# One full-array product for both heads' new state in a chunked RWKV-7 scan

## The chip, the cores and the metric

The kernel runs on one core of a Trainium2 chip, in one launch. The metric is device time in microseconds (us): the median of several runs, lower is better. The engines are TensorE (PE in the profile, with its weight loads as PEld), VectorE (DVE), ScalarE (ACT), GpSimd (POOL) and SyncE (SP), which here only issues DMAs.

## What is computed

One block of a streaming encoder over an input of 2048 frames by 1024 channels, float32. The normalised input is projected; its columns feed an RWKV-7 branch of 16 heads by 64, an S5 state-space branch, gates and merge gates. The part that matters here is the RWKV-7 recurrence:

```python
def frame_step(S, inp):
    r_t, w_t, k_t, v_t, a_t, b_t = inp
    sa = jnp.einsum('bhij,bhj->bhi', S, a_t)
    S = S * w_t[:, :, None, :] + sa[..., None] * b_t[:, :, None, :] + v_t[..., None] * k_t[:, :, None, :]
    return S, jnp.einsum('bhij,bhj->bhi', S, r_t)
```

It runs over 2048 frames for each head. The kernel does it in chunks of 64 frames.

## The kernel before

**Units and chunks.** A unit is a pair of heads `p` (8 pairs) and a block `tb` of 512 frames (4 blocks): 32 units, each of 8 chunks of 64 frames, so 256 chunks. The two heads of a pair lie on partitions 0 to 63 and 64 to 127 (`HS[0]`, `HS[1]`).

**A chunk in `scan`.** The tile `su[:, c]` (the profile calls it `SU`) is 128x128 and is the chunk's `cur`. On entry its diagonal 64x64 blocks hold the states of the two heads; the off-diagonal blocks hold the chunk's values, put there ahead by `prep2`: rows 64 to 127 of head 0's columns, rows 0 to 63 of head 1's. A chunk has three stages, with a `yield` between them:

1. `px` (L943): one product of 128x128 by 128 columns over both heads at once; DVE copies it to `rh`, ACT scales the old states into `us` (L948).
2. `po`, first half (L952): the states' part of the output, one product for each head on 64x64. `pu` (L955): the solved correction, one for each head on 64x64. It is scaled into `cur`, in place of the states: DVE writes head 0's diagonal block, ACT head 1's (L957).
3. `pn` (L961): the new state, one product for each head with weights `bt[:, c, h]` of 128x64 and the head's 64 columns of `cur`. DVE adds the decayed old state to it for each head (L969, and L72 for the one that goes through the helper `Woven`) and writes the diagonal block of the next chunk's tile. `po`, second half (L971): the rest of the output, one product for each head with weights `cur[:, HS[h]]` of 128x64; it has the same shape on the array as `pn`.

The weights `bt` are a tile of 8 chunks by 2 heads by 64 columns, made in `prep2`, so that the two heads' columns lie side by side. Products in f32 are two instructions each in the profile, a first and a second pass, each with a weight load.

**The order of the work.** The order on every engine is the order in which the code is written out; nothing is rescheduled. The main loop has 24 slots for each unit. Each slot takes one stage of `scan` for unit n, one piece of the preparation of later units (`prep1`, `prep2`), of `post1`, `sums` and `post2` for earlier ones, and then a share of `gm`, the stream of projections: six matmuls of 128x128 by 512 columns to a piece (L499 to L501, in f32 split into a high and a low part). So in TensorE's queue a chunk's stage stands between groups of projection matmuls, and after them come `pn` and `po` together. DVE's queue holds, beside the scan's steps, the splits of weights, the shifts of the projections, and the solve (L881, L885), which is woven in between other instructions.

**The run as a whole.** The scan fills some 140 to 2064 us of the run; the S5 branch, the GLU and the output projections follow.

Of the kernel before, what the change touches and what calls it, by code (L numbers as in the profile page):

```python
# [13 lines left out]
ALU = mybir.AluOpType  # L14
# [3 lines left out]
P = 128  # L18
# [5 lines left out]
C = 64  # L24
# [54 lines left out]
def tile_rwkv7_s5_block(  # L79
# [32 lines left out]
    pe, act, pool, sp = nc.tensor, nc.scalar, nc.gpsimd, nc.sync  # L112
    raw_dve = nc.vector
    dve = Woven(raw_dve)
    x = x[0]
    out = out[0]
# [34 lines left out]
    for i in range(2):  # L151
        for j in range(2):
            pool.affine_select(
                out=amask[64 * i:64 * i + 64, j, :], in_=amask[64 * i:64 * i + 64, j, :],
# [107 lines left out]
    if True:  # L262
# [14 lines left out]
        HS = (slice(0, 64), slice(64, 128))  # L277
# [656 lines left out]
        def scan(p, tb):  # L934
            n = f"_{p}_{tb}"
            u = U[p, tb]
            ar, at, r64, bt, decs, dd, su = (u[k] for k in ("ar", "at", "r64", "bt", "dec", "dd", "su"))
            po = u["po"] = pso.tile([P, TB], F32, tag="o", name="po" + n)
            for c in range(NC):
                dec = decs[:, c, :]  # L940
                cur = su[:, c, :]
                px = pst.tile([P, 512], F32, tag="st", name=f"px{n}_{c}")
                pe.matmul(px[:, 0:P], at[:, c, 0].rearrange("p h t -> p (h t)"), cur, start=True, stop=True)  # L943
                rh = sm.tile([P, P], F32, tag="rh", bufs=1, name=f"rh{n}_{c}")
                dve.tensor_copy(rh, px[:, 0:P])
                us = sm.tile([P, C], F32, tag="us", name=f"us{n}_{c}")
                for h in range(2):
                    act.activation(out=us[HS[h]], in_=cur[HS[h], HS[h]], func=AF.Copy, scale=dec[HS[h]])  # L948
                yield
                oc = po[:, c * C:(c + 1) * C]  # L950
                for h in range(2):
                    pe.matmul(oc[HS[h]], cur[HS[h], HS[h]], ar[HS[h], c, C:2 * C], start=True, stop=False)  # L952
                pu = pst.tile([P, 512], F32, tag="st", name=f"pu{n}_{c}")
                for h in range(2):
                    pe.matmul(pu[HS[h], 0:C], r64[HS[h], c, :], rh[HS[h], HS[h]], start=True, stop=True)  # L955
                dve.tensor_scalar(out=cur[0:64, 0:64], in0=pu[0:64, 0:C], scalar1=dd[0:64, c:c + 1], scalar2=None, op0=ALU.mult)
                act.activation(out=cur[64:128, 64:128], in_=pu[64:128, 0:C], func=AF.Copy, scale=dd[64:128, c:c + 1])  # L957
                yield
                pn = pst.tile([P, 512], F32, tag="st", name=f"pn{n}_{c}")
                for h in range(2):  # L960
                    pe.matmul(pn[HS[h], 0:C], bt[:, c, h, :], cur[:, HS[h]], start=True, stop=True)  # L961
                for h in range(2):
                    if c + 1 < NC:
                        nxt = su[HS[h], c + 1, HS[h]]
                    elif tb % 2 == 0:
                        nxt = U[p, tb + 1]["su"][HS[h], 0, HS[h]]
                    else:
                        nxt = ust[HS[h], p, :]
                    (raw_dve if h == 0 else dve).scalar_tensor_tensor(out=nxt, in0=pn[HS[h], 0:C], scalar=dec[HS[h]], in1=us[HS[h]], op0=ALU.mult, op1=ALU.add)  # L969
                for h in range(2):  # L970
                    pe.matmul(oc[HS[h]], cur[:, HS[h]], at[:, c, 1, h, :], start=False, stop=True)  # L971
                yield
# [559 lines left out]
        with tc.manual_schedule():  # L1532
# [13 lines left out]
            for n in range(-1, NU + 1):  # L1546
                credit = OFF if n == 0 else credit if n > NU - 2 else 0.0
                sc = scan(*units[n]) if 0 <= n < NU else none
                p2 = prep2(*units[n + 1]) if n + 1 < NU else none
                a = units[n + 2] if n + 2 < NU else None  # L1550
# [337 lines left out]
```

## Time and profile before

| | |
|---|---|
| Time, median of 3 runs | 2669.6 us (2667.75 to 2674.17) |
| The profiled execution | 2672.18 us, span 2670.3 us, granted clock 0.989 |
| PE busy | 2585.2 us (97%) |
| DVE busy | 1824.8 us (68%) |
| ACT busy | 1356.0 us (51%) |
| POOL busy | 536.5 us (20%) |

The span is the time from the first to the last instruction. The profile's groups put together instructions of one line, engine and shape; a form such as `128*64 128x64` is weights of 128 rows by 64 columns, and 128 partitions by 64 columns streamed past them. The rows of the timeline have a start in us from the span's beginning, a length in us and the instruction; neighbours of the same kind are merged, with their number behind the x. The end of a matmul is modelled, so lengths overlap; the distance between two starts is what a step costs. Where a row ends in brackets, the engine stood idle before it for so long, until the named instruction was done.

### The profile page before, as it was taken

To read this page: it belongs to the slowest core of one execution; us is meant where nothing else is said; L and a number is where in the kernel's file an instruction comes from. 1 tells how busy PE (TensorE), PEld (TensorE's weight loads), DVE (VectorE), ACT (ScalarE), POOL (GpSimd) and SP (SyncE) were. 2 spreads that over 40 slices of the span, in tenths; PEclk is the share of its full clock that TensorE was granted. 3 is DMA by queue.
4 is the path that set the end of the run, shared out by engine and by line. 5 is a ranking of instruction groups with operands and counts; after the bars stand their busy time and mean duration, and the time that the engine had idled before them with its cause. 6 is when DMAs were issued, how large, how long until landed. Compare 5 with 4: busy or idle time off the path is not lost.

```text
span 2670.3 us, 48574 instructions
## 1 busy us (share of the span) xinstructions
PE 2585.2 (97%) x17164; PEld 1969.7 (74%) x17164; DVE 1824.8 (68%) x5512; ACT 1356.0 (51%) x3441; POOL 536.5 (20%) x918
## 2 busy tenths in 40 slices
PE   7999999999999989999999999999989699999998
PEld 5777777777777767777777777777767488787887
DVE  6656677777667777767776767777767787554443
ACT  5455555555555677555555555555643443332111
POOL 2221212122112333221212122121321100210000
PEclk9999999999999999999999999999999799999999
DMA  4232323232333443332323233232465555664442
GB/s 129 77 84 65 101 78 102 69 93 81 86 86 95 136 123 104 98 82 78 91 76 96 78 91 90 79 92 74 145 173 155 166 155 146 205 212 145 140 141 95
DMA packets 255977, 294.58 MB, mean 110 GB/s; under 512 B 159505, under 2 KB 171894, under 8 KB 254710
## 3 DMA queue, kind: packets, MB, share of 16 engines
q1 hardware_dynamic: 212134, 147.80, 20.4%
q0 software_dynamic: 43600, 143.69, 17.6%
q8 instruction: 135, 2.21, 0.4%
q14 instruction: 108, 0.88, 0.1%
HBM read 206.80 MB, written 75.89 MB: 106 GB/s over the span
## 4 chain that ended last, share of the span: by engine, by line
PE 46%; DVE 6%; DMA 5%; issue 2%; ACT 2%; SPq 1%; POOL 0%; DVEq 0%; POOLq 0%; ACTq 0%
PE pout L1787 2%; PE pout L1786 2%; PE pout L1788 2%; PE ppa L499 1%; PE pma L499 1%; PE A L830 1%; PE pn L961 1%; PE ppa L500 1%; PE ppa L501 1%; DMA ce<-cw 1%; PE pma L500 1%; PE po L952 1%; PE pma L501 1%; PE pga L499 1%; PE pr L499 1%
## 5 line engine op out<-in xcount | busy, mean ns | idle before, releaser
L957 ACT ACTIVATE SU<-pu,dd 64x64 f32<-64x64 f32 x256 | 79.0, 309 | 368.1 <-DVE SU L72 276.4
L881 DVE TENSOR_TENSOR TM<-RF,IX 128x60 f32<-128x60 f32 (+24 forms) x992 | 207.3, 209 | 29.4 <-DMA IX<-ld 7.3
L885 DVE TENSOR_TENSOR RF<-RF,TM 128x60 f32<-128x60 f32 (+24 forms) x992 | 206.8, 208 | 27.2
L948 ACT ACTIVATE us<-SU,dec 64x64 f32<-64x64 f32 x512 | 176.4, 345 | 58.4 <-DVE SU L969 51.5
L72 DVE TENSOR_SCALAR SU<-pu,dd 64x64 f32<-64x64 f32 x256 | 69.9, 273 | 139.6 <-PE pu L955 60.6
L969 DVE SCALAR_TENSOR_TENSOR SU<-pn,dec,us 64x64 f32<-64x64 f32 x240 | 65.6, 273 | 117.7 <-PE pn L961 116.2
L72 DVE TENSOR_TENSOR AT<-A,amask 64x256 f32<-64x256 f32 (+1 forms) x256 | 102.2, 419 | 62.0 <-PE A L830 41.0
L835 ACT ACTIVATE AT<-A,dd 64x64 f32<-64x64 f32 x512 | 116.5, 302 | 46.6 <-PE A L830 41.4
L961 PEld LDWEIGHTS pn<-SU,BT 128*64 128x64 f32 x1024 | 55.9, 135 | 109.2 <-issue 39.5
L952 PEld LDWEIGHTS po<-AR,SU 64*64 64x64 f32 x1024 | 49.8, 131 | 94.8 <-issue 81.6
L72 DVE COPY rh<-px 128x128 f32<-128x128 f32 x256 | 74.1, 289 | 63.9 <-PE px L943 59.1
L499 PE MATMUL ppa<-yhi,whi_pa 128*128 128x512 f32 x256 | 116.3, 454 | 0.0
L943 PEld LDWEIGHTS px<-SU,AT 128*128 128x128 f32 x512 | 95.3, 189 | 27.1 <-DVE SU L72 6.2
L499 PE MATMUL pmb<-hhi,whi_mb 128*128 128x512 f32 x256 | 111.2, 435 | 0.0
L499 PE MATMUL pk<-hhi,whi_k 128*128 128x512 f32 x256 | 111.1, 434 | 0.0
L499 PE MATMUL pma<-hhi,whi_ma 128*128 128x512 f32 x256 | 111.1, 434 | 0.0
L499 PE MATMUL pga<-hhi,whi_ga 128*128 128x512 f32 x256 | 110.9, 433 | 0.0
L499 PE MATMUL pr<-hhi,whi_r 128*128 128x512 f32 x256 | 110.2, 430 | 0.0
L499 PE MATMUL pv<-hhi,whi_v 128*128 128x512 f32 x256 | 109.8, 429 | 0.3 <-ACT carry L452 0.3
L500 PE MATMUL ppa<-ylo,whi_pa 128*128 128x512 f32 x256 | 104.8, 409 | 3.0 <-DVE ylo L72 3.0
L961 PE MATMUL pn<-SU,BT 128*64 128x64 f32 x1024 | 94.5, 246 | 12.1 <-DVE SU L72 10.1
L501 PE MATMUL ppa<-yhi,wlo_pa 128*128 128x512 f32 x256 | 103.5, 404 | 0.6 <-DVE wlo_pa L72 0.6
(474 smaller groups left out, 7802.9 us busy)
## 6 DMA issues: line engine op xcount, KB each, us to landing
IX<-ld SPq DMA_DIRECT2D x128, 128.0 KB
raw_mb<-in_w_in_dram POOLq DMA_DIRECT2D x50, 256.0 KB, 3.7
raw_pa<-in_p_a_dram POOLq DMA_DIRECT2D x44, 256.0 KB, 3.9
raw_r<-in_w_in_dram POOLq DMA_DIRECT2D x36, 256.0 KB, 3.8
raw_k<-in_w_in_dram POOLq DMA_DIRECT2D x36, 256.0 KB, 4.0
raw_v<-in_w_in_dram POOLq DMA_DIRECT2D x36, 256.0 KB, 3.4
raw_ga<-in_w_in_dram POOLq DMA_DIRECT2D x34, 256.0 KB, 3.5
ce<-cw SPq DMA_DIRECT2D x16, 514.0 KB
```

The source lines that it names most:

```text
L72: r = f(*a, **kw)
L499: pe.matmul(ps, hi[:, k, :], xhi[:, kk_, :], start=(kk_ == 0), stop=False)
L500: pe.matmul(ps, hi[:, k, :], xlo[:, kk_, :], start=False, stop=False)
L501: pe.matmul(ps, lo[:, k, :], xhi[:, kk_, :], start=False, stop=(kk_ == 7))
L835: act.activation(out=at[HS[h], c, 0, h, :], in_=pas[h][HS[h], i, 0:C], func=AF.Copy, scale=dd[HS[h], c:c + 1])
L881: raw_dve.tensor_tensor(out=tm[:, 0:na, 0:nt], in0=rf[:, 0:na, s:s + 1].to_broadcast([P, na, nt]), in1=ix[:, s:s + 1, s + 1:32].to_broadca ...
L885: raw_dve.tensor_tensor(out=rf[:, 0:na, s + 1:32], in0=rf[:, 0:na, s + 1:32], in1=tm[:, 0:na, 0:nt], op=ALU.add)
L943: pe.matmul(px[:, 0:P], at[:, c, 0].rearrange("p h t -> p (h t)"), cur, start=True, stop=True)
L948: act.activation(out=us[HS[h]], in_=cur[HS[h], HS[h]], func=AF.Copy, scale=dec[HS[h]])
L952: pe.matmul(oc[HS[h]], cur[HS[h], HS[h]], ar[HS[h], c, C:2 * C], start=True, stop=False)
L957: act.activation(out=cur[64:128, 64:128], in_=pu[64:128, 0:C], func=AF.Copy, scale=dd[64:128, c:c + 1])
L961: pe.matmul(pn[HS[h], 0:C], bt[:, c, h, :], cur[:, HS[h]], start=True, stop=True)
```

## The change

The two products of `pn` become one. Its weights are both heads' columns of `bt` (128x128), and the whole `cur` is streamed past them, 128 columns. Of the 128x128 result the diagonal blocks are the new states; the two blocks off the diagonal, each head's weights with the other head's columns, are computed and not read. The DVE updates read the diagonal blocks, head 1's now 64 columns further on. `px`, `pu` and both parts of `po` are as before.

```diff
                 pn = pst.tile([P, 512], F32, tag="st", name=f"pn{n}_{c}")
-                for h in range(2):
-                    pe.matmul(pn[HS[h], 0:C], bt[:, c, h, :], cur[:, HS[h]], start=True, stop=True)
+                pe.matmul(pn[:, 0:P], bt[:, c].rearrange("p h k -> p (h k)"), cur, start=True, stop=True)
                 for h in range(2):
...
-                    (raw_dve if h == 0 else dve).scalar_tensor_tensor(out=nxt, in0=pn[HS[h], 0:C], scalar=dec[HS[h]], in1=us[HS[h]], op0=ALU.mult, op1=ALU.add)
+                    (raw_dve if h == 0 else dve).scalar_tensor_tensor(out=nxt, in0=pn[HS[h], HS[h]], scalar=dec[HS[h]], in1=us[HS[h]], op0=ALU.mult, op1=ALU.add)
                 for h in range(2):
                     pe.matmul(oc[HS[h]], cur[:, HS[h]], at[:, c, 1, h, :], start=False, stop=True)
```

On TensorE's queue, at the second chunk of the first unit, where the two heads' products stand between projections and `po`, it was:

```order
L500 MATMUL pga_0_1578<-hlo_179,whi_ga_0_1428 128x512
L501 MATMUL pga_0_1578<-hhi_178,wlo_ga_0_1429 128x512
L961 MATMUL pn_0_1_1614<-SU_0_1011,BT_0_950 64x64 [waits DVE_49]
L961 MATMUL pn_0_1_1614<-SU_0_1011,BT_0_950 64x64 [waits Activation_49]
L971 MATMUL po_0_1414<-AT_0_881,SU_0_1011 64x64 x2
L864 MATMUL pv_1_1622<-cen,zv_0_845 128x128 [waits PE_49]
```

And it is now, with lines one lower:

```order
L500 MATMUL pga_0_1577<-hlo_179,whi_ga_0_1428 128x512
L501 MATMUL pga_0_1577<-hhi_178,wlo_ga_0_1429 128x512
L960 MATMUL pn_0_1_1613<-SU_0_1011,BT_0_950 128x128 [waits Activation_49]
L970 MATMUL po_0_1414<-AT_0_881,SU_0_1011 64x64 x2
L864 MATMUL pv_1_1620<-cen,zv_0_845 128x128 [waits PE_49]
```

Head 0's product waited for DVE and head 1's for ACT; the one product waits for ACT, whose write of head 1's block stands behind DVE's write of head 0's. `po` keeps its place directly behind it. No other instruction moves on any engine.

## The prediction

> **What bounds the kernel now.** First the page's busy times, then the same by stretch (columns: stretch, its length, busy time of PE, weight loads, DVE, ACT and POOL with counts, granted clock, DMA share, GB/s).
>
> ```profile
> PE 2585.2 (97%) x17164; PEld 1969.7 (74%) x17164; DVE 1824.8 (68%) x5512; ACT 1356.0 (51%) x3441; POOL 536.5 (20%) x918
> ```
>
> ```profile
> 140.00:500.00 360.00, 359.12 (x2691) 268.39 (x2689) 250.21 (x836) 204.09 (x571) 75.74 (x128) 1.00 0.31 84
> 500.00:900.00 400.00, 399.54 (x2983) 299.35 (x2980) 285.15 (x960) 227.77 (x577) 88.06 (x151) 1.00 0.33 90
> 900.00:1060.00 160.00, 147.69 (x1079) 107.63 (x1077) 122.60 (x411) 116.58 (x326) 52.36 (x85) 0.99 0.43 122
> 1060.00:1240.00 180.00, 179.30 (x1333) 134.72 (x1332) 125.69 (x417) 102.52 (x301) 42.53 (x73) 1.00 0.33 89
> 1240.00:1710.00 470.00, 469.79 (x3535) 351.35 (x3533) 337.96 (x1117) 267.39 (x686) 97.19 (x169) 1.00 0.30 85
> 1710.00:2064.00 354.00, 343.73 (x2451) 255.03 (x2449) 257.11 (x943) 180.44 (x448) 85.46 (x144) 0.99 0.44 125
> ```
>
> The scan runs from 140 to 2064 us. In four of the six stretches, 1410 us of 1924, PE's rows leave 0.2 to 0.9 us uncovered: there TensorE's fixed order of work is the bound, and a nanosecond more on PE is a nanosecond more of time. Only 900 to 1060 (12.3 us idle) and 1710 to 2064 (10.3 us) have room.
>
> Next, what the changed product is today (groups by form).
>
> ```profile
> L943 PE MATMUL px<-SU,AT 128*128 128x128 f32 x512 | 99.4, 276 | 2.6 <-DVE SU L72 2.6
> L961 PE MATMUL pn<-SU,BT 128*64 128x64 f32 x1024 | 94.5, 246 | 12.1 <-DVE SU L72 10.1
> ```
>
> `pn` has 1024 records, so four for each of 256 chunks: two heads, two passes each. `px` (512, two per chunk) is what `pn` will be: f32, 128x128 weights, 128 columns, the same source tile `SU`. So the new product's price stands in this profile already. Busy times do not give it, because the ends of matmuls are modelled and overlap; starts do. A chunk's end with nothing waited for (columns: start, length, what):
>
> ```profile
> 1023.42 0.40 PE L501 MATMUL pga<-hhi,wlo_ga 128*128 128x512 f32 x1
> 1023.75 0.34 PE L961 MATMUL pn<-SU,BT 128*64 128x64 f32 x4
> 1023.92 0.29 PE L971 MATMUL po<-AT,SU 128*64 128x64 f32 x4
> 1024.13 0.50 PE L499 MATMUL pu<-hhi,whi_u 128*128 128x512 f32 x1
> ```
>
> From the last projection matmul to the next one: 0.71 us. Three things are to be seen. The step into `pn` is 0.33 us. All four passes of `pn` take 0.17 us, as the two heads, on different halves of the columns, run side by side. And `po`, the output product of the same chunk and the same half-array shape, follows with no gap.
>
> **The change part by part.** It removes four passes of 128*64 weights by 64 columns per chunk and adds two of 128*128 by 128 columns. `po` behind it stays on half the array. Nothing else is added; DMAs, ACT and DVE keep their instructions.
>
> *The step in.* The same step into a full-array f32 product:
>
> ```profile
> 1000.87 0.39 PE L501 MATMUL pk<-hhi,wlo_k 128*128 128x512 f32 x1
> 1001.10 0.38 PE L943 MATMUL px<-SU,AT 128*128 128x128 f32 x2
> 1001.24 0.48 PE L499 MATMUL pk<-hhi,whi_k 128*128 128x512 f32 x1
> ```
>
> 0.23 us, against 0.33: the weights are loaded under the projection. Here the change gains 0.10.
>
> *The step out.* After `pn` now comes a product on part of the array. One `px` in the trace is followed by such an operation directly (weights 128*32), and a group of four transposes on the full array is followed by `po` on 64*64:
>
> ```profile
> 2012.72 0.39 PE L501 MATMUL ppa<-yhi,wlo_pa 128*128 128x512 f32 x1
> 2012.95 0.38 PE L943 MATMUL px<-SU,AT 128*128 128x128 f32 x2
> 2013.26 1.05 PE L770 MATMUL sums<-ysq,selr 128*32 128x512 f32 x2
> ```
>
> ```profile
> 1019.83 0.60 PE L315 MATMUL tps<-ident,x 128*128 128x128 f32 x4
> 1020.36 0.33 PE L952 MATMUL po<-AR,SU 64*64 64x64 f32 x4
> ```
>
> 0.31 us from `px`'s first pass to the narrow operation. The transposes say the same: their four rows cover 0.60, the last of them some 0.28 (`px`'s mean), so one starts 0.11 after another, and of the 0.53 up to `po` 0.20 are left for the last step; 0.11 + 0.20 = 0.31. Against 1001.10 to 1001.24 (0.14, when the next operation is on the full array too) the change of shape costs 0.17. Today the pair `pn`, `po` pays that change once on the way in and once on the way out; after the change it pays it between `pn` and `po` and on the way out, so no change of shape is saved.
>
> *`po` alone.* For this a group with a wait in it is of use, where the passes stand apart:
>
> ```profile
> 1006.09 0.67 PE L961 MATMUL pn<-SU,BT 128*64 128x64 f32 x3
> 1006.50 0.27 PE L971 MATMUL po<-AT,SU 128*64 128x64 f32 x1
> 1006.60 0.22 PE L961 MATMUL pn<-SU,BT 128*64 128x64 f32 x1
> 1006.61 0.33 PE L971 MATMUL po<-AT,SU 128*64 128x64 f32 x3
> 1006.87 0.50 PE L499 MATMUL pv<-hhi,whi_v 128*128 128x512 f32 x1
> ```
>
> The first pass after a change of shape takes 0.11 (1006.50 to 1006.61) because its weights lie in the open; later ones take 0.06 (0.17 for `pn`'s two, less 0.11). `pn` and `po` together take 0.38 (1023.75 to 1024.13); without two passes of 0.06 `po` alone takes 0.26.
>
> *Sum for a chunk that waits for nothing:* before 0.33 + 0.38 = 0.71; after 0.23 + 0.31 + 0.26 = 0.80. Starts are rounded to 10 ns, so the loss is 0.08 to 0.11 us; I take 0.095, as the transposes' rows lean a little above. Times 256: **+24.3 us**.
>
> A page weighs in. The Trainium skill, "TensorE: Matmul & The Clock Gate", section "Back-to-back issue gap", gives some 81 ns per matmul of 128 columns for a stream of load and matmul pairs. By it the new product's first pass would take 0.08, not the 0.11 of the rows, and the sum would be some 7 us smaller. The rows decide, since they hold the very operation.
>
> *Chunks that wait.* Both heads now wait for the later half of `SU`: DVE scales the upper half, ACT the lower. In the group above head 0 started at 1006.09; head 1 had to wait for ACT:
>
> ```profile
> 1006.49 0.13 PEld L961 LDWEIGHTS pn<-SU,BT 128*64 128x64 f32 x1 [0.21 <-ACT SU L957]
> ```
>
> It followed 0.40 later, and from there to the projection took 0.38. Afterwards the whole product starts there, and with its weights in the open, as this waiting `px` shows:
>
> ```profile
> 1018.10 0.49 PE L943 MATMUL px<-SU,AT 128*128 128x128 f32 x2 [0.42 <-DVE SU L72]
> 1018.34 0.48 PE L499 MATMUL pga<-hhi,whi_ga 128*128 128x512 f32 x1
> ```
>
> 0.24 instead of 0.14, so 0.10 more: 0.31 + 0.10 + 0.26 = 0.67 against 0.38, a loss of 0.29, which is 0.195 above the loss already counted. How many wait (waits of `pn`'s weight loads: releaser, us, times; the whole run first, then 900 to 1060):
>
> ```profile
>   DVE SU L72: 30.1, 33
>   ACT SU L957: 4.4, 21
> ```
>
> ```profile
>   DVE SU L72: 7.9, 13
>   ACT SU L957: 1.7, 8
> ```
>
> 33 at most: 33 x 0.195 = **+6.4 us**.
>
> *What waits give back.* The first `px` of two successive units of eight chunks:
>
> ```profile
> 1407.52 0.38 PE L943 MATMUL px<-SU,AT 128*128 128x128 f32 x2
> 1465.84 0.38 PE L943 MATMUL px<-SU,AT 128*128 128x128 f32 x2
> ```
>
> 58.32 us for a unit, 7.3 for a chunk. A wait whose end PE does not set shrinks by what PE has lost before it. In the four full stretches there is nothing to shrink. The other two, 514 us, hold some 70 chunks at that pace: 70 x 0.095 = 6.7 us there, and the 6.4 above. Between none and all 13 us comes back; I take **-5**, nearer the low end, because DVE's lateness itself often goes back to an operand that PE made a chunk or two earlier.
>
> *The update behind the product.* DVE's two updates wait for `pn` today:
>
> ```profile
> L969 DVE SCALAR_TENSOR_TENSOR SU<-pn,dec,us 64x64 f32<-64x64 f32 x240 | 65.6, 273 | 117.7 <-PE pn L961 116.2
> 1008.80 0.39 PE L943 MATMUL px<-SU,AT 128*128 128x128 f32 x2
> ```
>
> In a chunk without waits the result ends 0.67 after the last projection start today (1023.75 + 0.34 less 1023.42) and 0.61 afterwards (by `px`, 1001.10 + 0.38 less 1000.87), so slightly earlier: nothing. In a waiting one it ends 0.49 after 1006.49 instead of 0.33, and both updates, 0.27 each, stand behind it: done near 1007.6, with `px` of the next chunk at 1008.80, behind a projection. DVE's queue loses 0.4 us there 33 times at 68% busy. I cost it at nothing; the cover is those six projection matmuls, and where it is gone, `px` is late next.
>
> *Sum:* 24.3 + 6.4 - 5 = +25.7. The profiled execution took 2672.2 us (2670.3 of it the span), which gives 2697.9; the median of the runs is 2.6 below that execution, so **2695**.
>
> **The rivals.**
> *The step out is free (faster).* If `po`'s weights were loaded under `pn`'s second pass, the step from the second pass to `po` would be 0.06, and a chunk would take 0.23 + 0.11 + 0.06 + 0.26 = 0.66: 0.05 x 256 = 12.8 less, 2657. It decides from a step below about 0.10. The Trainium skill's page on TensorE has a rule for it (Part 2, step by step: weight loads are pulled ahead of matmuls in flight where they go to the background buffer); its page "TensorEngine Tiling (Array Packing)", Key Properties, says that a change of mode drains the array. The row at 2013.26 and the one at 1020.36 have 0.20. Chance 0.05.
> *The waits give all of it back (no change).* All of `pn`'s waits for `SU` are 34.5 us, enough in sum. Against it stands the steady part, where PE has 0.2 us free in 470. It would end at 2670 to 2677. Chance 0.07.
> *More chunks come to wait (slower still).* One wait on the later head, and both updates behind one product, lengthen the chain from chunk to chunk by 0.4 us where it is tight. Were 66 more chunks to wait, three times today's number, 66 x 0.195 = 13 would come on top: 2708. For it: heads are 0.40 apart when DVE is late. Against: 223 of 256 chunks do not wait for a half of `SU` today, and the product's result comes no later in them. Chance 0.12.
>
> **How the numbers follow.** The forecast, a loss on every chunk with a little given back, has 0.74; what is left, 0.02, is for the unforeseen on either side. Its own range: 186 chunks in the full stretches at 0.08 give +15 (2685), everything at 0.11 with no wait giving back gives 28 + 6 = +34 (2704). Taking in part of the third rival and some of the second: 2683 to 2707. A measurement here tells 0.3%, 8 us. Slower 0.87, same 0.07, faster 0.06.
>
> **What the profile after would show.** Right: `pn` as 512 records of 128*128 by 128; projection to `pn` 0.23, `pn` to `po` 0.31, `po` to projection 0.26; a unit in the steady part at 58.32 + 8 x 0.095 = 59.1 us; busy time of DVE and ACT unchanged. Wrong: a step from `pn` to `po` under 0.2, a steady unit still at 58.3, or `px` waiting for `SU` more often than some 20 times.

## The result, and the profile after

The changed kernel takes 2693.02 us (median of 6 runs, 2692.18 to 2696.01), the kernel before 2671.56 us (6 runs, 2666.07 to 2674.17): 1.0088 of it, with a 95% interval of 1.0077 to 1.0099. It is slower by 21 us by the medians and by some 23 by the ratio; 2695 us, 25.7 more, had been forecast. The profiled execution's span went from 2670.3 to 2691.6 us.

The page's busy times and the groups of the two full-array products after the change:

```profile
PE 2609.8 (97%) x16652; PEld 2029.4 (75%) x16652; DVE 1825.6 (68%) x5512; ACT 1355.3 (50%) x3441; POOL 536.3 (20%) x918
...
L960 PE MATMUL pn<-SU,BT 128*128 128x128 f32 x512 | 101.9, 281 | 17.0 <-ACT SU L957 16.7
L943 PE MATMUL px<-SU,AT 128*128 128x128 f32 x512 | 99.1, 275 | 1.8 <-DVE SU L72 1.7
```

PE has 512 matmuls fewer and is busy 25 us longer; DVE, ACT and POOL do what they did. `pn`'s busy time of 101.9 us, against 94.5 before, shows little of the loss, because the loss lies in steps between starts. A chunk that waits for nothing, and one that waits, from the timeline after:

```profile
1049.02 0.39 PE L501 MATMUL plora<-hhi,wlo_lora 128*128 128x512 f32 x1
1049.25 0.38 PE L960 MATMUL pn<-SU,BT 128*128 128x128 f32 x2
1049.57 0.34 PE L970 MATMUL po<-AT,SU 128*64 128x64 f32 x4
1049.83 0.50 PE L499 MATMUL plora<-hhi,whi_lora 128*128 128x512 f32 x1
```

```profile
1042.58 0.49 PE L960 MATMUL pn<-SU,BT 128*128 128x128 f32 x2 [0.46 <-ACT SU L957]
1043.00 0.34 PE L970 MATMUL po<-AT,SU 128*64 128x64 f32 x4
1043.26 1.05 PE L718 MATMUL pss<-onec,sq 128*128 128x2 f32 x8
```

The first takes 0.23 + 0.32 + 0.26 = 0.81 us from projection to projection, where it was 0.71; the second 0.68 from the start of `pn`. Where PE has no room, a unit of eight chunks shows it (first `px` of two units that follow one another; before, there were 58.32 us between two such rows):

```profile
1603.14 0.27 PE L943 MATMUL px<-SU,AT 128*128 128x128 f32 x1
1662.30 0.27 PE L943 MATMUL px<-SU,AT 128*128 128x128 f32 x1
```

59.16 us, so 0.84 more for a unit, 0.105 for a chunk. Over 256 chunks that is 26.9 us, over 31 units 26.0. The scan from the first unit's `px` to the last unit's, 31 units, lost less. Before and after:

```profile
137.29 0.38 PE L943 MATMUL px<-SU,AT 128*128 128x128 f32 x2
...
903.39 0.38 PE L943 MATMUL px<-SU,AT 128*128 128x128 f32 x2
...
1049.12 0.38 PE L943 MATMUL px<-SU,AT 128*128 128x128 f32 x2
...
2005.98 0.38 PE L943 MATMUL px<-SU,AT 128*128 128x128 f32 x2
```

```profile
138.55 0.38 PE L943 MATMUL px<-SU,AT 128*128 128x128 f32 x2
...
916.63 0.38 PE L943 MATMUL px<-SU,AT 128*128 128x128 f32 x2
...
1060.62 0.38 PE L943 MATMUL px<-SU,AT 128*128 128x128 f32 x2
...
2029.92 0.27 PE L943 MATMUL px<-SU,AT 128*128 128x128 f32 x1
```

From first to last it is 1868.69 us and 1891.37, so +22.7. The two units from 903 to 1049, where PE had 12 us of idle time, took 145.73 before and 143.99 after: they got shorter by 1.7 instead of longer by 1.7. The other 29 units lost 24.4, which is 29 times 0.84. So in sum the time came back in those two units; which wait gave it back the rows do not show. A few us between two single executions are not firm either: the run with the heads swapped, below, has the steady unit of the kernel before, 58.32 us (1407.11 to 1465.43), and took 1864.70 us over the same 31 units (138.46 to 2003.16), 4.0 less than that kernel.

### The profile page after: what moved, and what is told of

It is laid out like the page before. It is cut to its first block, busy times and chain, and to the rows that moved or that the text cites. A ratio compares the mean times of both kernels' runs of the same rounds, so it can differ in the third digit from the quotient of the medians.

```text
span 2691.6 us, 47548 instructions
## 1 busy us (share of the span) xinstructions
PE 2609.8 (97%) x16652; PEld 2029.4 (75%) x16652; DVE 1825.6 (68%) x5512; ACT 1355.3 (50%) x3441; POOL 536.3 (20%) x918
## 4 chain that ended last, share of the span: by engine, by line
PE 47%; DVE 5%; DMA 5%; issue 2%; ACT 2%; SPq 1%; POOL 0%; DVEq 0%; POOLq 0%; ACTq 0%
PE pout L1786 2%; PE pout L1785 2%; PE pout L1787 2%; PE ppa L499 2%; PE pma L499 1%; PE ppa L500 1%; PE A L830 1%; PE ppa L501 1%; PE pga L499 1%; PE po L970 1%; PE pn L960 1%; PE po L952 1%; PE pma L500 1%; PE pma L501 1%; PE pr L499 1%
## 5 line engine op out<-in xcount | busy, mean ns | idle before, releaser
L957 ACT ACTIVATE SU<-pu,dd 64x64 f32<-64x64 f32 x256 | 79.0, 309 | 370.2 <-DVE SU L72 280.7
L960 PEld LDWEIGHTS pn<-SU,BT 128*128 128x128 f32 x512 | 93.7, 189 | 49.6 <-ACT SU L957 30.7
L960 PE MATMUL pn<-SU,BT 128*128 128x128 f32 x512 | 101.9, 281 | 17.0 <-ACT SU L957 16.7
```

The costliest lines, as they stand in the source:

```text
L960: pe.matmul(pn[:, 0:P], bt[:, c].rearrange("p h k -> p (h k)"), cur, start=True, stop=True)
```

## The experiments

Three theories stood against one another. *Shape change:* between `pn` on the whole array and `po` on half of it TensorE pays a change of shape at every chunk. *Size:* the full-array product is dearer in itself. *Wait:* both heads now wait for ACT's half of the state, and the updates come later. Each ratio below is against runs of the kernel before that were taken together with the run (medians 2666.64, 2668.77 and 2665.97 us).

**Without `po`, halves and full.** Both the kernel before and the changed one lose the second output product, so that nothing narrow stands behind `pn` but what follows it anyway (the first output product then closes its sum with `stop=True`, a line left out of this cut and of the next one like it):

```diff
-                for h in range(2):
-                    pe.matmul(oc[HS[h]], cur[:, HS[h]], at[:, c, 1, h, :], start=False, stop=True)
```

> The kernel before (two half-array products of pn) with the second output product po (L971) left out; it leaves that part of the output undone. It is the baseline of the next run. Shape-change theory: pn alone stays on half the array, and a chunk loses only po's two later passes, 0.06 us each: 0.71 goes to 0.59, times 256 about -30 us, near 2641 us. Size theory (the full-array product is dearer in itself) and wait theory (both heads wait for ACT's half) say the same here.

> The changed kernel (one full-array pn) with the same po left out, so that a projection of the same array shape follows pn. Shape-change theory: 0.23 in, 0.11 first pass, 0.03 out, and the step to the second projection matmul 0.31 instead of 0.34: 0.37 for a chunk instead of 0.59, so some 60 us below the run without po on halves, near 2580. Size theory: the full product still costs 0.1 us more than the halves: some 24 us above that run, near 2665. Wait theory: above that run too, by some 20 us.

Measured: 2647.76 us with halves (0.992 of before, 0.9906 to 0.9934), 2623.96 with the full product (0.984, 0.9823 to 0.9856). Without `po` the full product is some 21 to 24 us faster than the halves (by the ratios, by the medians); with it, it is 21 to 23 slower. That rules the size theory out, and it speaks against the wait theory, since both heads wait for ACT here too. Of the 60 us expected less than half came. A group with halves, one with the full product, and the waits of the full product's weight loads (us in total, times, the longest):

```profile
1306.97 0.40 PE L501 MATMUL pga<-hhi,wlo_ga 128*128 128x512 f32 x1
1307.30 0.34 PE L961 MATMUL pn<-SU,BT 128*64 128x64 f32 x4
1307.57 0.50 PE L499 MATMUL pga<-hhi,whi_ga 128*128 128x512 f32 x1
```

```profile
1340.05 0.39 PE L501 MATMUL pv<-hhi,wlo_v 128*128 128x512 f32 x1
1340.28 0.38 PE L960 MATMUL pn<-SU,BT 128*128 128x128 f32 x2
1340.42 0.48 PE L499 MATMUL pv<-hhi,whi_v 128*128 128x512 f32 x1
```

```profile
PEld pn L960 <- ACT SU L957: 44.6, 63, 4.6
```

The halves cost 0.60 and the full product 0.37, as expected. At the full product PE's weight loads wait for ACT's half 63 times, 44.6 us; with halves they wait for DVE's half 23 times, 22.5 us, and for ACT's 20 times, 4.2. The weight loads of `px` wait for the state 39 times, 21.4 us, against 20 times, 10.2. That is some 29 us more of waiting, out of 36 to 39 that are missing. It would mean that, as PE's part shrinks, the chain from `pu` over DVE and ACT to `pn` is no longer covered; no run tests this. I had also left out that behind 62 chunks another narrow operation (`A`, the solve's `pr`) follows, where the step out stays.

**The other head first.** The kernel before, with both heads made to wait for ACT:

```diff
-                for h in range(2):
+                for h in (1, 0):
                     pe.matmul(pn[HS[h], 0:C], bt[:, c, h, :], cur[:, HS[h]], start=True, stop=True)
```

> The kernel before, with the two half-array products of pn written in the other order, head 1 (which needs ACT's block) ahead of head 0, so that both wait for ACT as the one product does and DVE's first update comes as late. Wait theory: most of the 23 us appears, near 2690. Shape-change and size theory: nothing measurable, 2669 to 2674, since at a chunk that doesn't wait the four passes run side by side in either order and only some 33 chunks wait.

Measured: 2667.61 us, 0.9998 (0.9989 to 1.0008). The weight loads of `pn` wait for ACT's half 50 times here, 36.1 us, where in the kernel before they wait for DVE's 24 times, 20.0 us, and for ACT's 21 times, 4.4. Waiting for the later half costs nothing that can be measured. The wait theory falls for half-array products.

**`po` on the full array too, first try.** The second output product as one full-array product into the free columns of `pn`'s bank, behind DVE's updates:

```diff
-                for h in range(2):
-                    pe.matmul(oc[HS[h]], cur[:, HS[h]], at[:, c, 1, h, :], start=False, stop=True)
+                pe.matmul(pn[:, P:2 * P], cur, at[:, c, 1].rearrange("p h t -> p (h t)"), start=True, stop=True)
```

> The changed kernel with po's second half as one full-array product too (weights the whole chunk tile, 128 columns), written beside pn in its bank and not added to the output, so that part of the output is missing. Shape-change theory: no change of shape between pn and po nor behind po: 0.23 + three steps of 0.11 + 0.03 = 0.59 and 0.31 for the next step, against 0.71 and 0.34 before: -0.145 x 256 = -37 us, near 2634. Size theory: two full products in place of halves cost twice 0.1 us: some +47 us against before, near 2718. Wait theory: as the changed kernel, near 2693.

Measured: 2926.76 us, 1.0975 (1.0955 to 1.0995), which fits none of the three. The timeline and the waits tell why:

```profile
1306.91 0.38 PE L960 MATMUL pn<-SU,BT 128*128 128x128 f32 x2
1307.99 0.49 PE L969 MATMUL pn<-AT,SU 128*128 128x128 f32 x2 [0.69 <-DVE SU L72]
1308.23 0.48 PE L499 MATMUL pu<-hhi,whi_u 128*128 128x512 f32 x1
```

```profile
PE pn L969 <- DVE SU L72: 203.5, 240, 5.9
```

The second product writes to the tile that DVE's two updates still read, so TensorE stands still until both are done, at every chunk: 240 times, 203.5 us, and 16 times more, 13.0 us, at the last chunks of units that write the state to `ust`. It says nothing on the theories and was put right in the next run.

**`po` on the full array, ahead of the updates.** The same product, written directly behind `pn`.

> As the run with po's second half as a full-array product (again written beside pn and missing from the output), but issued directly behind pn, ahead of the updates that read pn, so that TensorE doesn't wait for these reads. Shape-change theory: 0.23 + three steps of 0.11 + 0.03 = 0.59, next projection step 0.31; at the 62 chunks where another narrow operation follows (A and the solve's pr), the step out stays 0.20. 194 x -0.145 + 62 x 0.05 = -25 us against before if PE alone binds; the run without po showed that about half of such a gain comes back as waits for the states, so 2641 to 2655. Size theory: above the changed kernel, 2690 or more.

Measured: 2659.92 us, 0.9973 (0.9961 to 0.9984). Two full-array products are faster than two pairs of halves, and by some 31 us faster than one of each (1.0088 less 0.9973). Where a projection follows, the steps came as forecast:

```profile
1320.59 0.39 PE L501 MATMUL pgb<-hhi,wlo_gb 128*128 128x512 f32 x1
1320.82 0.38 PE L960 MATMUL pn<-SU,BT 128*128 128x128 f32 x2
1321.04 0.39 PE L961 MATMUL pn<-AT,SU 128*128 128x128 f32 x2
1321.18 0.48 PE L499 MATMUL pgb<-hhi,whi_gb 128*128 128x512 f32 x1
1321.50 0.40 PE L500 MATMUL pgb<-hlo,whi_gb 128*128 128x512 f32 x1
```

Steps of 0.23, 0.22 and 0.14, 0.59 in sum, and 0.32 for the next. The time missed the forecast by some 5 us on the slow side. The forecast counted all chunks but 62 like this one; behind some 60 more stands `pv` or `pss` instead of a projection, and the step out to `pv` is 0.23 (1307.71 to 1307.94 in that run). The weight loads of `pn` wait for ACT's half 57 times there, 45.0 us.

**`po` in another place.** The changed kernel, with a chunk's second output product moved into the next chunk's second stage, which is on half-array shapes already; the output is complete:

```diff
+            def second(c):
+                for h in range(2):
+                    pe.matmul(po[HS[h], c * C:(c + 1) * C], su[:, c, HS[h]], at[:, c, 1, h, :], start=False, stop=True)
...
                 yield
+                if c:
+                    second(c - 1)
                 oc = po[:, c * C:(c + 1) * C]
...
-                for h in range(2):
-                    pe.matmul(oc[HS[h]], cur[:, HS[h]], at[:, c, 1, h, :], start=False, stop=True)
+                if c == NC - 1:
+                    second(c)
```

> The changed kernel with po's second half moved: a chunk's part is issued in the next chunk's second stage, ahead of po's first half and pu, which are narrow already (128x64 in front of 64x64); the last chunk of a unit keeps its place. The output is complete. Shape-change theory: pn alone costs 0.37 with 0.31 behind it instead of 0.80 and 0.34; the second stage grows by 0.12 if 128x64 and 64x64 weights count as one shape on the array, by some 0.27 if they don't. Against before that is about -49 us or -11 us with PE alone binding, and half of it with waits: 2645 or 2665. Size theory: no faster than the changed kernel less nothing, about 2690.

Measured: 2656.48 us, 0.9954 (0.9937 to 0.997): faster than both kernels. The stage of `pn`, and the stage that took `po` in:

```profile
1303.57 0.39 PE L501 MATMUL pga<-hhi,wlo_ga 128*128 128x512 f32 x1
1303.80 0.38 PE L966 MATMUL pn<-SU,BT 128*128 128x128 f32 x2
1303.93 0.47 PE L499 MATMUL pga<-hhi,whi_ga 128*128 128x512 f32 x1
...
1321.82 0.34 PE L941 MATMUL po<-AT,SU 128*64 128x64 f32 x4
1322.09 0.33 PE L958 MATMUL po<-AR,SU 64*64 64x64 f32 x4
1322.25 0.28 PE L961 MATMUL pu<-rh,R 64*64 64x64 f32 x4
```

Alone, the full product costs 0.36 from projection to projection. In the second stage, 128*64 weights ahead of 64*64 cost 0.27, where four passes of 64*64 ahead of more 64*64 cost 0.16: the two half-array shapes are not one shape either. By its rows it is the dearer of the two cases expected; the 12 us gained are about what that case gives with PE alone binding (11), so little seems to have come back as waits, though no run shows that by itself.

**The halves of the state apart.** In the kernel before, ACT's write at L957 waits for DVE's 168 times, 276.4 us; both read one PSUM tile, `pu`. With one tile for each head ACT waits only for the product `pu` itself; the output is complete. It was done to the kernel before, to the changed one and to the one with `po` moved:

```diff
-                pu = pst.tile([P, 512], F32, tag="st", name=f"pu{n}_{c}")
+                pu = [pst.tile([P, 512], F32, tag="st", name=f"pu{h}{n}_{c}") for h in range(2)]
```

> The kernel before with pu's two heads in two PSUM tiles instead of one, so that ACT's write of head 1's block of the state no longer stands behind DVE's write of head 0's; the output is complete. Only chunks that wait for the later half gain, some 30 of 256 with 0.3 us at most: 2660 to 2670, by every theory. It is the baseline for the next run.

> The changed kernel with pu's two heads in two PSUM tiles; the output is complete. If waiting for both halves is what the change costs, its distance to the run with halves and pu apart falls to a few us, as the two halves now come at about the same time. Shape-change theory: the distance stays at some 22 to 27 us (0.107 x 256 less what waits give back), near 2685 to 2690, since the step from pn to po is paid at every chunk.

> The kernel that moves po's second half into the next chunk's second stage, with pu's two heads in two PSUM tiles; the output is complete. Its projection-to-projection excursion at pn has a median of 0.21 us and a mean of 0.25 over two projection starts, the rest being waits for ACT's half; with the halves apart most of those go: 2645 to 2653, below every kernel so far that keeps the output. Size theory: no lower than the run with halves and pu apart.

Measured: halves 2662.16 us (0.9982, 0.997 to 0.9994); full 2681.13 (1.0071, 1.0052 to 1.009); `po` moved 2654.84 (0.9962, 0.9948 to 0.9976). The waits of `pn`'s weight loads for ACT's half, in the changed kernel and then with the tiles apart; and the first `px` of two successive units with the tiles apart, with halves and then with the full product:

```profile
PEld pn L960 <- ACT SU L957: 30.7, 37, 5.3
```

```profile
PEld pn L960 <- ACT SU L957: 5.7, 6, 1.4
```

```profile
1405.20 0.38 PE L943 MATMUL px<-SU,AT 128*128 128x128 f32 x2
1463.52 0.38 PE L943 MATMUL px<-SU,AT 128*128 128x128 f32 x2
```

```profile
1474.73 0.38 PE L943 MATMUL px<-SU,AT 128*128 128x128 f32 x2
1533.89 0.38 PE L943 MATMUL px<-SU,AT 128*128 128x128 f32 x2
```

The waits for ACT's half are all but gone (with the waits that stand under other names now, the loads of `pn` still wait 17.6 us in all), and the full product still stands 0.0089 above the halves (1.0071 less 0.9982), as it did with them (0.0088). That is 24 us by the ratios and 19 by the medians, where 22 to 27 were expected. The steady unit takes 58.32 us with halves and 59.16 with the full product, 0.84 more, exactly as with one tile. The waits are not what the change costs. The last run missed its forecast: the waits of `pn`'s weight loads for ACT's half fell from 24.9 us to 7.1 there too, but against the kernel before it is no faster than with `po` moved alone (0.9962 and 0.9954, intervals overlapping). Part of these waits only changed their name: in all, the loads of `pn` waited 24.9 us and then 17.8. `px`'s weight loads wait for the state somewhat more, 15.2 us against 13.3. The rest I did not settle.

## Why the prediction was right

*The step in.* Forecast 0.23 in place of 0.33, by `px`'s row; measured 0.23. That the new product's price already stood in the profile, under another name, was the base of the whole forecast.

*The step out.* Forecast 0.31 from `pn` to `po`, from the one `px` that had a narrow operation behind it; measured 0.32 in the row above. The rival in which this step is free, and the run ends near 2657, fell with it. Where the time goes, the weight loads show, before (at the group of 1023.42) and after (at that of 1049.02):

```profile
1023.86 0.20 PEld L971 LDWEIGHTS po<-AT,SU 128*64 128x64 f32 x4
```

```profile
1049.03 0.42 PEld L960 LDWEIGHTS pn<-SU,BT 128*128 128x128 f32 x2
1049.56 0.20 PEld L970 LDWEIGHTS po<-AT,SU 128*64 128x64 f32 x4
```

Before, the loads of `po` began 0.06 ahead of `po` itself (1023.92), under `pn`. After, `pn`'s own loads begin 0.22 ahead of it, under the projection, but those of `po` begin only with `po`, at 1049.56. Of the 0.32, `pn`'s first pass is 0.11 and the second 0.21, where a second pass takes 0.03 when a projection of the same shape follows (1321.04 to 1321.18 in the run with both products full, less 0.11). The Trainium skill, "TensorEngine Tiling (Array Packing)", Key Properties, says that a change of mode drains the array; the rows fit that, but that the wait of 0.21 is a drain no run shows.

*`po` alone.* Forecast 0.26; measured 0.26. Its 0.11 was read as the first pass after a change of shape, but in the group at 1006.09 `pn` and `po` have one shape: it is a first pass whose weights were not loaded ahead. After the change `po`'s weights are not loaded ahead either, and the price came out the same.

*The sum for a chunk.* 0.095 was taken, from starts rounded to 10 ns; the unit's length shows 0.105. Over 256 chunks the term was 24.3 and should have been 26.9.

*Chunks that wait.* 0.67 forecast, 0.68 measured for the group at 1042.58. Their number was misread: the 33 waits put together those of weight loads (24 times, 20.0 us) and of matmuls (9 times, 10.1 us), so that one wait can count twice; in the same way the 34.5 us of the second rival are 24.4 for the loads. After the change the weight loads of `pn` wait for ACT's half 37 times, 30.7 us. So 33 came near by luck: with 24 the term would have been +4.7, with 37 +7.2.

*What waits give back.* Forecast -5 against +6.4 for the chunks that wait, together +1.4. Measured over 31 units, the two together are -3.3 (22.7 less 26.0); one cannot be told from the other. In sum all of it came in the stretch from 903 to 1049, where more came back than the chunks lost there. So this term was mis-sized by some 5 us, though two executions of one pace differ by 4.0 over the scan. The chunk's term was too small by 2.6 and this one too high, so the two misses partly cancel: that the 25.7 forecast stands so near 22.7 in those 31 units, 21.3 in the whole span and 21 to 23 in the runs is in part luck. That the steps between starts set the loss is not.

*The cover behind the product* held: `px`'s weight loads wait for the state less than before (8 times, 4.6 us, against 12 times, 6.2 us), and DVE's and ACT's busy times did not move.

*The 81 ns* that the Trainium skill, "TensorE: Matmul & The Clock Gate", section "Back-to-back issue gap", gives for a matmul of 128 columns would have made the sum some 7 us smaller. Here such a pass takes 0.11 (two in 0.22, from 1320.82 to 1321.04 in the run with both products full). The measured unit has the sum larger, not smaller; the rows of `px` were the better source.

## What to carry to other kernels

Count the changes of shape on TensorE before counting matmuls: two half-array products that run side by side, and share their shape with what stands behind them, can be cheaper than one full-array product with a narrow one behind it. A product of the new shape often stands in the profile already under another line; read the step into it and the step from it to each kind of neighbour, from starts and not from busy times. If a product is to go to the full array, move or widen its narrow neighbour with it, as the run with `po` in the next chunk's stage did.

## What the runs showed of the hardware that was not expected

Two half-array shapes are not one: 128*64 followed by 64*64 costs some 0.1 us more than 64*64 followed by 64*64 (0.27 and 0.16 for four passes up to the next product). In these rows the weights of a product of another shape are not loaded ahead: behind the full-array `pn`, `po`'s loads begin together with `po` itself, some 0.2 us after `pn`'s second pass began, where `pn`'s loads begin 0.22 us ahead of it under the projection. And a product that writes unused columns of a PSUM tile, while another engine reads other columns of it, waits for that reader in this program, 216.5 us in sum over 256 chunks; whether the chip needs that order, the runs do not show.
